# Attention scores of a hybrid encoder block on 64-row tiles of TensorE, without a padded copy of the keys

## The chip, the cores and the metric

The kernel runs on one core of a Trainium2 chip. The metric is the device time of one execution in microseconds (us). A core has five engines with an instruction queue each: TensorE (PE, the matrix array of 128 rows by 128 columns; a matmul contracts over the rows), VectorE (DVE), ScalarE (ACT), GpSimd (POOL) and SyncE (SP, which here only starts transfers). They run side by side and wait for each other on semaphores; each takes its own instructions strictly in the order in which they stand. SBUF is the memory on the core, 128 partitions wide; PSUM holds the results of matmuls in eight banks of 512 fp32 columns by 128 partitions.

## The reference

One layer of an encoder on 512 tokens of width 1024, all in fp32: a norm, one wide projection, attention and retention as two branches, gates, a merge, an output projection, and then a mixture of 64 experts. What the change touches is the attention: three groups of 8 heads, 64 numbers a head, rotary positions on queries and keys. Cut to that:

```python
ATTN_PAIRS = ((128, 1), (512, 4), (2048, 16))   # (window, dilation)
q_a = apply_rotary(q_a.reshape(B, S, n_a, HEAD_DIM), cos, sin)
k_a = apply_rotary(k_a.reshape(B, S, n_a, HEAD_DIM), cos, sin)
...
for g, (window, dilation) in enumerate(ATTN_PAIRS):
    o, l = dilated_window_attention(q_a[:, :, g], k_a[:, :, g], v_a[:, :, g], dilation, window // (2 * dilation))
...
    scores = jnp.einsum('nhbqd,nhbkd->nhbqk', qb, kw) * (Dh ** -0.5)
    scores = jnp.where(valid[None, None], scores, -jnp.inf)
    m = jnp.max(scores, axis=-1, keepdims=True)
    p = jnp.exp(scores - m)
    denom = jnp.sum(p, axis=-1, keepdims=True)
    out = jnp.einsum('nhbqk,nhbkd->nhbqd', p, vw) / denom
```

Group 0 looks at a block of 64 keys and its neighbours (192 keys a query block). Groups 1 and 2 look at every 4th or 16th token. The group outputs are summed, weighted by their denominators.

## The kernel before

**Projections.** The weights of the wide projection (w_in) come in pieces of 512 KB (`raw`), two buffers, loaded by SyncE (L109). ScalarE rounds each to a high half `wH` (L228) and VectorE takes the rest `wL` (L229), three buffers each. A product is then three matmuls: L293, L294 and L295 with the tokens in columns, L299, L300 and L301 with the weights in columns. They add up in the four `acc` banks of PSUM. All of this is called "projection" below; 0.233 us apart, these matmuls fill TensorE whenever nothing else stands in its queue.

**Keys and queries.** `rotary_to` takes a projected bank to SBUF (L331), copies it with the halves of each head swapped (`sw`, by DMA), and multiplies (VectorE L343, GpSimd L344). The sum of the two is done by GpSimd: in place for the queries (L346), and for the keys into `kP` (L350), a copy in which the two heads that share 128 partitions are set apart: head z keeps its 64 partitions in plane z, and the other 64 partitions of that plane hold zeros, put there once (L598).

**Scores.** Two heads share the 128 partitions, the first in partitions 0 to 63, the second in 64 to 127. With `kP`, one matmul over all 128 rows gives the scores of both heads: the zeros keep them apart. In group 0 (`windows`) a slot is such a pair of heads. For each of 4 tiles of 128 queries and each of 4 slots there are two matmuls (L640), one for each block of 64 queries; each fills 64 columns of the array and streams 2 x 192 keys into one PSUM bank. In groups 1 and 2 a half tile has 4 heads: two matmuls (L684) of 128 queries by 2 x 128 keys.

**Behind the scores.** `probs` lets VectorE add the mask and find the minimum (L604), and ScalarE take the exponential (L606). `transposed_probs` transposes by matmul into the same bank (L610), and VectorE copies to SBUF (L612). Matmuls with the values follow (AV: L650 and L655 in group 0, L696 in groups 1 and 2). ScalarE copies their banks into a record (L658, L698). Records of groups 1 and 2 go to DRAM (`scr`) and come back in the order of tokens (`rb`); `combine` weights and sums the three (L741, L744, L747) while the gate projections run. Four PSUM banks, `tmp`, serve scores, transposes and AV.

**Retention** stands ahead of the attention. Its scores (L546) are matmuls over 64 rows, with the two heads of a pair in PSUM banks of their own.

**Order.** The order in each engine's queue is fixed when the program is built, by a scheduler that follows the dependences and its own estimates of times; it mixes projections of what comes next between the attention's small matmuls. Behind the attention come four branch gates (`branch_gate`, evacuated by ScalarE at L715), the merge and the output projection. Then the experts: all 64 are streamed from memory in tiles of 2 MB (L981: `wa`, `wB`, `we`, `x`). The first of these, `we`, is loaded from ScalarE's queue; the SBUF it takes overlaps the end of group 0's record, so it waits for the last use of that record in `combine`.

## Time and profile before

| | |
|---|---|
| median of 3 runs | 1605.37 us (1605.3 to 1606.52) |
| profiled execution | 1605.17 us |
| its span, first to last instruction | 1603.3 us |
| busy: PE, DVE, ACT, POOL | 1337.7, 562.9, 316.0, 204.4 us |
| mean granted TensorE clock over the span | 0.917 |
| HBM read, written | 459.96 MB, 4.26 MB |

Busy shares are means over the span, and the span has stages with different limits, so they don't tell what bounds the kernel; that is read by stage. PE is a pipeline: one matmul's record overlaps the next one's, so the cost of a matmul in a stream is the distance from its start to the next start, not its duration. An fp32 matmul leaves two records. PEld, the loading of weights into the array, overlaps PE.

### The profile page before, as it was taken

The page shows a single profiled execution, that of the slowest core. Times are in us where ns is not written, and L with a number is a line of the kernel's source. Part 1 is how long each engine was busy: PE and PEld are TensorE (multiplying, and loading weights), DVE is VectorE, ACT ScalarE, POOL GpSimd, SP SyncE. Part 2 cuts the span into 40 slices and gives each one's busy share as a digit, 9 for nine tenths or more (in the row PEclk, how much of TensorE's full clock was granted, in tenths as well). Part 3 has the DMA queues.
Part 4 walks back from the last instruction along what each step waited for, and adds up shares of the span by engine and source line. Part 5 has one row for each costly group of instructions (what it writes and reads, how often), then busy time and mean ns, then how long its engine had stood idle before and what let it go on. Part 6 is the DMA issues. An engine that isn't in the chain of part 4 may idle for free.

```text
span 1603.3 us, 21137 instructions
## 1 busy us (share of the span) xinstructions
PE 1337.7 (83%) x8821; PEld 818.5 (51%) x8821; DVE 562.9 (35%) x1227; ACT 316.0 (20%) x605; POOL 204.4 (13%) x154
## 2 busy tenths in 40 slices
PE   8999999999999999998776776776686677677684
PEld 7788786697978788752331331332232232233133
DVE  7557564475847335541221121121021021022013
ACT  5332333334353423210000000000000000000002
POOL 2203352260715011000000000000000000000002
PEclk9999999999999999997997897998888887898887
DMA  4434253243434324999999999999999999999995
GB/s 168 123 92 106 93 145 93 56 121 105 113 108 155 123 92 176 376 409 427 429 428 428 427 430 426 428 427 430 426 428 430 427 428 430 426 428 428 428 428 238
DMA packets 70547, 476.14 MB, mean 297 GB/s; under 512 B 14192, under 2 KB 14320, under 8 KB 45680
## 3 DMA queue, kind: packets, MB, share of 16 engines
q1 hardware_dynamic: 68400, 471.46, 73.5%
q10 hardware_dynamic: 2048, 3.29, 0.6%
q8 instruction: 71, 1.16, 0.3%
q14 instruction: 28, 0.23, 0.0%
HBM read 459.96 MB, written 4.26 MB: 290 GB/s over the span
## 4 chain that ended last, share of the span: by engine, by line
PE 50%; DMA 39%; DVE 8%; issue 1%; ACT 1%; POOL 1%; SPq 0%; DVEq 0%; ACTq 0%; POOLq 0%
DMA wa<-in_moe_w2r_dram 14%; DMA x<-in_moe_w2r_dram 10%; DMA we<-in_moe_w2r_dram 9%; PE tmp L814 6%; PE acc L294 6%; PE acc L295 6%; PE acc L293 6%; PE acc L1018 5%; PE acc L300 3%; PE acc L301 3%; PE acc L299 3%; PE acc L1100 3%; PE tmp L1073 2%; DMA wa<-in_moe_w_dram 2%; DMA wB<-in_moe_w2c_dram 2%; DVE wL L229 2%
## 5 line engine op out<-in xcount | busy, mean ns | idle before, releaser
L1018 PE MATMUL acc<-wa,xT 128*32 128x512 f32 x1200 | 160.2, 669 | 74.5 <-DMA wa<-in_moe_w_dram 74.5
L229 DVE SCALAR_TENSOR_TENSOR wL<-raw,nwx,wH 128x512 fp32r<-128x512 f32 x152 | 150.7, 1025 | 104.2 <-ACT wH L228 102.7
L293 PE MATMUL acc<-x,wH 128*128 128x512 f32 x416 | 169.5, 407 | 1.1 <-ACT v L715 1.1
L295 PE MATMUL acc<-x,wL 128*128 128x512 f32 x416 | 167.4, 403 | 0.0
L294 PE MATMUL acc<-x,wH 128*128 128x512 f32 x416 | 167.0, 401 | 0.0
L228 ACT ACTIVATE wH<-raw,nwx 128x512 fp32r<-128x512 f32 x152 | 103.2, 717 | 173.7 <-PE acc L301 64.7
L299 PE MATMUL acc<-wH,x 128*128 128x512 f32 x320 | 127.7, 399 | 2.0 <-ACT rt L585 1.5
L1018 PEld LDWEIGHTS acc<-wa,xT 128*32 128x32 f32 x1200 | 36.1, 115 | 181.2 <-DMA wa<-in_moe_w_dram 92.9
L1100 PE MATMUL acc<-wa,hid 128*32 128x512 f32 x480 | 84.0, 834 | 52.1 <-DMA wa<-in_moe_w2r_dram 50.0
L301 PE MATMUL acc<-wH,x 128*128 128x512 f32 x320 | 127.1, 397 | 0.2 <-DVE x L216 0.2
L300 PE MATMUL acc<-wL,x 128*128 128x512 f32 x320 | 126.9, 397 | 0.0
L1160 POOL TENSOR_TENSOR wa<-big,wf 128x256 f32<-128x256 f32 x12 | 8.4, 733 | 899.0 <-DMA wB<-in_moe_w2c_dram 895.6
L1050 DVE SCALAR_TENSOR_TENSOR hid<-hid,gsl,acc 128x512 f32<-128x512 f32 x16 | 12.0, 747 | 303.2 <-ACT hid L1049 171.8
L814 PE MATMUL tmp<-oh,h 128*128 128x128 f32 x960 | 111.2, 277 | 0.3 <-DVE big L1084 0.3
L814 PEld LDWEIGHTS tmp<-oh,h 128*128 128x128 f32 x960 | 108.3, 192 | 4.7 <-DVE big L1084 4.7
L1063 DVE TENSOR_TENSOR yp<-acc,yp 128x512 fp32r<-128x512 f32 (+1 forms) x34 | 22.3, 656 | 245.8 <-ACT yp L1062 245.8
L293 PEld LDWEIGHTS acc<-x,wH 128*128 128x128 f32 x416 | 78.7, 189 | 21.2 <-issue 2.4
L295 PEld LDWEIGHTS acc<-x,wL 128*128 128x128 f32 x416 | 78.5, 189 | 19.9 <-issue 2.4
L294 PEld LDWEIGHTS acc<-x,wH 128*128 128x128 f32 x416 | 78.4, 188 | 18.6 <-issue 1.8
L1073 PE MATMUL tmp<-yp 128*128 128x512 f32 (+1 forms) x272 | 77.4, 421 | 4.6 <-ACT yp L1062 2.0
L1084 DVE TENSOR_TENSOR big<-big,tmp 128x512 f32<-128x512 f32 (+1 forms) x128 | 74.9, 646 | 16.0 <-PE tmp L1073 16.0
L299 PEld LDWEIGHTS acc<-wH,x 128*128 128x128 f32 x320 | 68.2, 213 | 13.7 <-ACT rt L585 2.4
(274 smaller groups left out, 1603.3 us busy)
## 6 DMA issues: line engine op xcount, KB each, us to landing
wa<-in_moe_w_dram SPq DMA_DIRECT2D x75, 2048.0 KB, 39.0
wa<-in_moe_w2r_dram SPq DMA_DIRECT2D x30, 2048.0 KB, 35.8
x<-in_moe_w_dram SPq DMA_DIRECT2D x25, 2048.0 KB, 39.1
raw<-in_w_in_dram SPq DMA_DIRECT2D x76, 512.0 KB, 3.6
x<-in_moe_w2r_dram SPq DMA_DIRECT2D x15, 2048.0 KB, 39.0
wB<-in_moe_w_dram SPq DMA_DIRECT2D x15, 2048.0 KB, 39.0
we<-in_moe_w2r_dram SPq DMA_DIRECT2D x10, 2048.0 KB, 38.4
we<-in_moe_w_dram SPq DMA_DIRECT2D x10, 2048.0 KB, 39.0
```

Of the source, the lines that this page charges most:

```text
L228: nc.scalar.activation(wH[:, k, :], raw[:, k, :], AF.Copy, scale=sc)
L229: nc.vector.scalar_tensor_tensor(wL[:, k, :], raw[:, k, :], sc, wH[:, k, :], op0=ALU.mult, op1=ALU.subtract)
L293: nc.tensor.matmul(ps[tt], wh[:, cs], srcH.blk(kt), **fl)
L294: nc.tensor.matmul(ps[tt], wh[:, cs], srcL.blk(kt), start=False, stop=False)
L295: nc.tensor.matmul(ps[tt], wl[:, cs], srcH.blk(kt), start=False, stop=(kt == nk - 1))
L299: nc.tensor.matmul(ps[tt], aH, wh, **fl)
L300: nc.tensor.matmul(ps[tt], aH, wl, start=False, stop=False)
L301: nc.tensor.matmul(ps[tt], aL, wh, start=False, stop=(kt == nk - 1))
L814: nc.tensor.matmul(gp[j // 4][:, (j % 4) * P:(j % 4 + 1) * P], h[:, t, j * P:(j + 1) * P], oh_t.rearrange("p e c -> p (e c)"), start=(t == ...
L1018: nc.tensor.matmul(p_[e * CAP:(e + 1) * CAP, :], xT[:, j, e * CAP:(e + 1) * CAP], wt[:, w_, e, :], start=(j == 0), stop=(j == NK - 1))
L1073: nc.tensor.matmul(pss[t], ohT[:, t * P:(t + 1) * P], y[:, cs], start=(i == 0), stop=(i == 1))
L1100: nc.tensor.matmul(py[hf][e * CAP:(e + 1) * CAP, :], hdT[:, i, e * CAP:(e + 1) * CAP], wt[:, e, hf * 512:(hf + 1) * 512], start=(i == 0), ...
```

## The change

`kP` and its zero fill go. The keys' rotary sum is done in place, like that of the queries. Scores are taken over the 64 rows of one head, by two 64-row tiles of the array, and the two heads of a pair write to PSUM banks of their own (`pair[0]`, `pair[1]`). In group 0 two slots share a pair of banks: 8 matmuls (quarters of the array, 192 keys each), then four heads' `probs`, and the transposes of each slot go back into one bank of the pair. In groups 1 and 2 a tile's 8 heads share a pair: 8 matmuls, `pair[i]` with the four heads of parity i; the record's copy (L705) becomes strided. The lines of after.py stand up to 10 lower or 8 higher than those of before: scores L635 and L686, probs L594 and L596, transposes L600, copy L602, AV L651, L656 and L703, gates L723, expert loads L989.

```diff
--- before.py
+++ after.py
@@ -342,12 +341,7 @@
                 w3 = w.rearrange("p (r l) -> p r l", r=4) if dilated else w
                 nc.vector.tensor_tensor(d3, d3, order(ropeT[:, 0, :]), op=ALU.mult)
                 nc.gpsimd.tensor_tensor(w3, w3, order(ropeT[:, 1, :]), op=ALU.mult)
-                if pad is None:
-                    (adder or nc.gpsimd).tensor_tensor(d, d, w, op=ALU.add)
-                else:
-                    for z in range(2):
-                        hp = slice(z * HD, (z + 1) * HD)
-                        nc.gpsimd.tensor_tensor(pad[hp, b - 1 + k, z, :], d[hp], w[hp], op=ALU.add)
+                (adder or nc.gpsimd).tensor_tensor(d, d, w, op=ALU.add)
         return evac
 
     def qk_tiles():
...
@@ -592,10 +586,6 @@
     scr = [dram.tile([S, REC], F32, name=f"scr{g}") for g in (1, 2)]
     at = right.enter_context(tc.tile_pool(name="at", bufs=1, side="right"))
     rec0 = at.tile([P, NT, REC], F32, name="rec0")
-
-    kP = at.tile([P, 4, 2, S], F32, name="kP")
-    for z in range(2):
-        nc.gpsimd.memset(kP[(1 - z) * HD:(2 - z) * HD, :, z, :], 0.0)
     orders = (nat, dil4, dil4)
 
     def probs(rec, hh, ps, sm, mask):
...
@@ -634,14 +625,24 @@
             po_ps = [tmp(), tmp()]
             for slot in range(4):
                 hh = 2 * slot
-                ps = tmp()
-                sm = rp.tile([P, 512], F32, name="sd", bufs=6)
-                for qs, k0 in parts_:
-                    nc.tensor.matmul(ps[qs, :2 * W], qT[:, slot, t * P + qs.start:t * P + qs.stop],
-                                     kP[:, slot, :, k0:k0 + W], start=True, stop=True)
-                for i in range(2):
-                    cs = slice(i * W, (i + 1) * W)
-                    probs(rec, hh + i, ps[:, cs], sm[:, cs], masks[:, mo_:mo_ + W])
+                if slot % 2 == 0:
+                    pair = [tmp(), tmp()]
+                    sms = []
+                    for u in range(2):
+                        for qs, k0 in parts_:
+                            for i in range(2):
+                                hp = slice(i * HD, (i + 1) * HD)
+                                nc.tensor.matmul(pair[i][qs, u * W:(u + 1) * W],
+                                                 qT[hp, slot + u, t * P + qs.start:t * P + qs.stop],
+                                                 kT[hp, slot + u, k0:k0 + W], start=True, stop=True)
+                    for u in range(2):
+                        sm = rp.tile([P, 512], F32, name="sd", bufs=6)
+                        sms.append(sm)
+                        for i in range(2):
+                            cs = slice(i * W, (i + 1) * W)
+                            probs(rec, hh + 2 * u + i, pair[i][:, u * W:(u + 1) * W], sm[:, cs],
+                                  masks[:, mo_:mo_ + W])
+                ps, sm = pair[slot % 2], sms[slot % 2]
                 prT = transposed_probs(ps, sm, 3)
                 oc = slice(slot * (HD + 1), (slot + 1) * (HD + 1))
                 for i in range(2):
@@ -661,7 +662,7 @@
     for g in range(3):
         qT, kT = qk_tiles()
         project_in(512 * g, None, rotary_to(qT, g > 0))
-        project_in(1536 + 512 * g, None, rotary_to(kT, g > 0, kP))
+        project_in(1536 + 512 * g, None, rotary_to(kT, g > 0))
         vt = rp.tile([P, 2080], F32, name="v", bufs=3)
         v4 = vt.rearrange("p (t h d) -> p t h d", t=NT, h=NH)
         nc.gpsimd.memset(v4[:, :, :, HD:HD + 1], 1.0)
...
         if g == 0:
-            windows(qT, v4)
+            windows(qT, kT, v4)
             continue
         for t in range(NT):
             rec_t = at.tile([P, REC], F32, name="rec", bufs=4)
             rec = rec_t[:, :]
-            for h0 in range(0, NH, 4):
-                ps = tmp()
+
+            ts = slice(t * P, (t + 1) * P)
+            pair = [tmp(), tmp()]
+            for x in range(4):
+                for i in range(2):
+                    hp = slice(i * HD, (i + 1) * HD)
+                    nc.tensor.matmul(pair[i][:, x * P:(x + 1) * P], qT[hp, x, ts], kT[hp, x, ts], start=True,
+                                     stop=True)
+            sms = []
+            for i in range(2):
                 sm = rp.tile([P, 512], F32, name="sd", bufs=6)
-                ts = slice(t * P, (t + 1) * P)
-                for i in range(0, 4, 2):
-                    nc.tensor.matmul(ps[:, i * P:(i + 2) * P], qT[:, (h0 + i) // 2, ts], kP[:, (h0 + i) // 2, :, ts],
-                                     start=True, stop=True)
-                for i in range(4):
-                    cs = slice(i * P, (i + 1) * P)
-                    probs(rec, h0 + i, ps[:, cs], sm[:, cs],
+                sms.append(sm)
+                for x in range(4):
+                    cs = slice(x * P, (x + 1) * P)
+                    probs(rec, 2 * x + i, pair[i][:, cs], sm[:, cs],
                           masks[:, 3 * HD:3 * HD + P] if g == 1 else masks[:, 9 * HD:])
-                prT = transposed_probs(ps, sm, 4)
+            for i in range(2):
+                prT = transposed_probs(pair[i], sms[i], 4)
                 po_ps = tmp()
-                for i in range(4):
-                    oc = i * (HD + 1)
+                for x in range(4):
+                    oc = x * (HD + 1)
                     for f in range(2):
-                        qs = slice(i * P + f * HD, i * P + (f + 1) * HD)
-                        nc.tensor.matmul(po_ps[f * HD:(f + 1) * HD, oc:oc + HD + 1], prT[:, qs], v4[:, t, h0 + i, :],
-                                         start=True, stop=True)
-                nc.scalar.copy(rec[:, h0 * (HD + 1):(h0 + 4) * (HD + 1)], po_ps[:, :4 * (HD + 1)])
+                        qs = slice(x * P + f * HD, x * P + (f + 1) * HD)
+                        nc.tensor.matmul(po_ps[f * HD:(f + 1) * HD, oc:oc + HD + 1], prT[:, qs],
+                                         v4[:, t, 2 * x + i, :], start=True, stop=True)
+                nc.scalar.copy(rec[:, :NH * (HD + 1)].rearrange("p (x z w) -> p x z w", x=4, z=2)[:, :, i],
+                               po_ps[:, :4 * (HD + 1)].rearrange("p (x w) -> p x w", x=4))
             nc.sync.dma_start(out=scr[g - 1].rearrange("(l r) c -> r l c", r=4)[t], in_=rec)
 
 
```

The change lets the scheduler order the queues anew up to the output projection; the first scores stand behind the same 414 projections as before. Three places.

TensorE, local stage, two successive slots of one tile of queries, before (L640 scores, L610 transposes, L650 and L655 AV, L293 to L295 projections):

```order
L640 MATMUL tmp<-kP,qT 64x384
L610 MATMUL tmp<-ident,sd 128x128 x3
L640 MATMUL tmp<-kP,qT 64x384
L295 MATMUL acc<-x_133,wL 128x512
L293 MATMUL acc<-x_133,wH 128x512
L294 MATMUL acc<-x_133,wH 128x512
L295 MATMUL acc<-x_133,wL 128x512
L650 MATMUL tmp<-v,sd 64x65 x4
L655 MATMUL tmp<-v,sd 64x65 x4
L640 MATMUL tmp<-kP,qT 64x384
L610 MATMUL tmp<-ident,sd 128x128 x3
L640 MATMUL tmp<-kP,qT 64x384
```

And now the beginning of a group of two slots (L635 scores, L600 transposes, L651 AV):

```order
L635 MATMUL tmp<-kT,qT 64x192 x8
L293 MATMUL acc<-x_132,wH 128x512
L294 MATMUL acc<-x_132,wH 128x512
L295 MATMUL acc<-x_132,wL 128x512
L293 MATMUL acc<-x_132,wH 128x512
L294 MATMUL acc<-x_132,wH 128x512
L295 MATMUL acc<-x_132,wL 128x512
L600 MATMUL tmp<-ident,sd 128x128 x4
L293 MATMUL acc<-x_133,wH 128x512
L600 MATMUL tmp<-ident,sd 128x128 x2
L294 MATMUL acc<-x_133,wH 128x512
L651 MATMUL tmp<-v,sd 64x65 x4
```

The transposes that stood between the two halves of a slot's scores stand behind six projections, and the scores of two slots stand together. Over the stage, before: 7 of the 16 slots have transposes between their two matmuls and 9 don't; 108 projections; 37 islands (unbroken stretches without a projection). Now: 8 groups of 8 score matmuls, 74 projections, 28 islands. The first group is followed by 13 projections, the others by 6.

TensorE, a dilated stage, a half of a tile of queries before (L684 scores, L610 transposes):

```order
L684 MATMUL tmp<-kP,qT 128x256 x2
L293 MATMUL acc<-x_132,wH 128x512
L294 MATMUL acc<-x_132,wH 128x512
L295 MATMUL acc<-x_132,wL 128x512
L293 MATMUL acc<-x_132,wH 128x512
L294 MATMUL acc<-x_132,wH 128x512
L295 MATMUL acc<-x_132,wL 128x512
L610 MATMUL tmp<-ident,sd 128x128 x3
L293 MATMUL acc<-x_132,wH 128x512
L610 MATMUL tmp<-ident,sd 128x128
L294 MATMUL acc<-x_132,wH 128x512
L295 MATMUL acc<-x_132,wL 128x512
```

And a tile now (L686 scores, L600 transposes):

```order
L686 MATMUL tmp<-kT,qT 128x128 x8
L295 MATMUL acc<-x_132,wL 128x512
L293 MATMUL acc<-x_132,wH 128x512
L294 MATMUL acc<-x_132,wH 128x512
L295 MATMUL acc<-x_132,wL 128x512
L293 MATMUL acc<-x_132,wH 128x512
L600 MATMUL tmp<-ident,sd 128x128 x3
L294 MATMUL acc<-x_132,wH 128x512
L600 MATMUL tmp<-ident,sd 128x128
L295 MATMUL acc<-x_132,wL 128x512
L600 MATMUL tmp<-ident,sd 128x128 x2
L293 MATMUL acc<-x_132,wH 128x512
```

Two blocks of scores with 6 to 10 projections behind each became one with 5 (in each stage's first tile 6), and the transposes of the second bank follow those of the first ahead of the first AV matmuls. Each of the two stages has 95 and 101 projections before and 55 now; the two together have 54 islands before and 48 now. The projections that left stand behind the stages: from the last AV matmuls of the second dilated stage to the next small matmuls there are 211 before and 257 now.

ScalarE, the load of `we` and what stands around it, before (L715 evacuates the second gate, `wH` is the rounding of weights; numbers tell buffers apart):

```order
L715 ACTIVATE kT_3973<-acc_3974,bg_63 128x512
L715 ACTIVATE kT_3973<-acc_3975,bg_63 128x512
L715 ACTIVATE kT_3973<-acc_3976,bg_63 128x512
L228 ACTIVATE wH_4217<-raw_4215,nwx_77 128x512
L715 ACTIVATE kT_3973<-acc_3977,bg_63 128x512
L228 ACTIVATE wH_4217<-raw_4215,nwx_77 128x512
L981 DMA we_5652<-in_moe_w13_dram 128x4096
L228 ACTIVATE wH_4261<-raw_4259,nwx_77 128x512 x2
```

And now (L723 is the gates' evacuation):

```order
L228 ACTIVATE wH_4125<-raw_4123,nwx_77 128x512 x2
L228 ACTIVATE wH_4178<-raw_4176,nwx_77 128x512 x2
L989 DMA we_5701<-in_moe_w13_dram 128x4096
L723 ACTIVATE kT_4022<-acc_4023,bg_63 128x512
L723 ACTIVATE kT_4022<-acc_4024,bg_63 128x512
L723 ACTIVATE kT_4022<-acc_4025,bg_63 128x512
L723 ACTIVATE kT_4022<-acc_4026,bg_63 128x512
L228 ACTIVATE wH_4222<-raw_4220,nwx_77 128x512 x2
L228 ACTIVATE wH_4266<-raw_4264,nwx_77 128x512 x2
```

The load stood behind the four evacuations of this gate; now it stands ahead of them, and two pieces of weights fewer are rounded ahead of it. On TensorE, 137 projections stand between the last AV matmul of the second dilated stage and the first matmul of the third gate, which takes a bank that the first of these evacuations empties; the first matmul with `wH_4222` stands 24 further on.

## Rows read from the trace of the kernel before

**Rows 1.** The page's slices: 40 equal slices of the span (40.1 us each); busy tenths of PE, the granted clock in tenths, busy tenths of the DMA engines, and GB/s.

```profile
span 1603.3 us, 21137 instructions
...
PE 8999999999999999998776776776686677677684
...
PEclk9999999999999999997997897998888887898887
DMA  4434253243434324999999999999999999999995
GB/s 168 123 92 106 93 145 93 56 121 105 113 108 155 123 92 176 376 409 427 429 428 428 427 430 426 428 427 430 426 428 430 427 428 430 426 428 428 428 428 238
```

**Rows 2.** Windows of the trace (the local stage, the first dilated stage, and all from 640 us on): stretch in us, its length, then busy time and instructions of PE, PEld, DVE, ACT and POOL, the granted clock, the DMA share and GB/s.

```profile
249.00:313.00 64.00, 64.00 (x479) 37.27 (x479) 27.91 (x92) 25.18 (x56) 5.04 (x5) 1.00 0.29 79
...
355.00:395.00 40.00, 40.00 (x290) 30.98 (x290) 18.23 (x80) 20.60 (x53) 2.44 (x2) 1.00 0.32 100
...
640.00:1604.00 964.00, 707.81 (x5498) 315.36 (x5496) 192.02 (x494) 68.16 (x153) 11.73 (x18) 0.86 0.98 417
```

**Rows 3.** Timeline of SyncE's queue around the start of the experts' stream: start and length in us, queue, line, transfer.

```profile
629.02 0.34 SPq L981 DMA_DIRECT2D wa<-in_moe_w_dram  x1
...
641.92 1.41 SPq L981 DMA_DIRECT2D wa<-in_moe_w_dram  x3
```

**Rows 4.** Groups of instructions by line and shape, from 140 to 620 us: line, engine, operation, tiles, partitions x elements, count, busy us, mean ns of one, idle time ahead.

```profile
L350 POOL TENSOR_TENSOR kP<-kT,sw 64x512 f32<-64x512 f32 x24 | 39.9, 1662 | 1.3
...
L346 POOL TENSOR_TENSOR qT<-qT,sw 128x512 f32<-128x512 f32 x12 | 20.5, 1725 | 4.8 <-issue 2.6 <-DVE qT L343 2.2
L606 ACT ACTIVATE sd<-sd,rec 128x128 f32<-128x128 f32 x64 | 20.5, 391 | 10.8 <-DVE rec L604 10.8
L640 PE MATMUL tmp<-kP,qT 128*64 128x384 f32 x64 | 18.9, 505 | 0.0
...
L606 ACT ACTIVATE sd<-sd,rec 128x192 f32<-128x192 f32 x32 | 12.8, 447 | 25.9 <-DVE rec L604 25.9
```

**Rows 5.** Timeline of PE in the local stage: start and length in us, line, tiles, shape, and how many records (two a matmul of fp32 scores).

```profile
257.25 1.51 PE L640 MATMUL tmp<-kP,qT 128*64 128x384 f32 x8
258.69 0.50 PE L293 MATMUL acc<-x,wH 128*128 128x512 f32 x1
259.03 0.39 PE L294 MATMUL acc<-x,wH 128*128 128x512 f32 x1
...
261.74 0.86 PE L640 MATMUL tmp<-kP,qT 128*64 128x384 f32 x2
262.53 0.55 PE L610 MATMUL tmp<-ident,sd 128*128 128x128 f32 x3
263.00 0.86 PE L640 MATMUL tmp<-kP,qT 128*64 128x384 f32 x2
263.79 0.50 PE L295 MATMUL acc<-x,wL 128*128 128x512 f32 x1
```

**Rows 6.** The same view in the first dilated stage.

```profile
369.16 0.40 PE L295 MATMUL acc<-x,wL 128*128 128x512 f32 x1
369.49 0.69 PE L696 MATMUL tmp<-v,sd 128*64 128x65 f32 x16
370.10 1.13 PE L684 MATMUL tmp<-kP,qT 128*128 128x256 f32 x4
370.88 0.58 PE L293 MATMUL acc<-x,wH 128*128 128x512 f32 x1
371.30 0.39 PE L294 MATMUL acc<-x,wH 128*128 128x512 f32 x1
...
372.23 0.40 PE L295 MATMUL acc<-x,wL 128*128 128x512 f32 x1
```

**Rows 7.** The same view in the retention, its scores and the projection behind them.

```profile
122.86 1.16 PE L546 MATMUL tmp<-kT 64*128 64x128 f32 x16
123.95 0.51 PE L299 MATMUL acc<-wH,x 128*128 128x512 f32 x1
```

**Rows 8.** Timeline of VectorE and of ScalarE behind the scores of rows 6.

```profile
371.27 0.29 DVE L604 CUSTOM_DVE_ANT_0 sd<-tmp,masks 128x128 f32<-128x128 f32 x1 [1.93 <-PE tmp L684]
...
371.49 0.28 DVE L604 CUSTOM_DVE_ANT_0 sd<-tmp,masks 128x128 f32<-128x128 f32 x1
...
371.67 1.28 ACT L606 ACTIVATE sd<-sd,rec 128x128 f32<-128x128 f32 x4 [1.07 <-DVE rec L604]
```

**Rows 9.** The chain of waits ahead of the second dilated stage: start and length in us, what.

```profile
434.48 7.38 DVE wL L229 x4
```

**Rows 10.** Timeline of PE in the third gate, where it waits; in brackets the idle time that the record shows ahead of it.

```profile
527.22 0.50 PE L293 MATMUL acc<-x,wH 128*128 128x512 f32 x1 [1.05 <-ACT v L715]
```

**Rows 11.** Timeline of ScalarE from the last dilated record copy to the load of `we`.

```profile
482.39 0.38 ACT L698 COPY rec<-tmp 128x260 f32<-128x260 f32 x1
...
504.82 0.71 ACT L228 ACTIVATE wH<-raw,nwx 128x512 fp32r<-128x512 f32 x1
514.82 0.33 ACTq L981 DMA_DIRECT2D we<-in_moe_w_dram  x1
```

**Rows 12.** The chain of waits behind that load.

```profile
515.36 8.52 DMA raw<-in_w_in_dram
```

More of the change, by code (lines that the diff above doesn't have):

```diff
@@ L321, in transposed, with rotary_to @@
         nc.scalar.copy(dst[:, :, tt * P:(tt + 1) * P], pt.rearrange("p (b t) -> p b t", b=4))
-    def rotary_to(dst, dilated, pad=None, adder=None):
+    def rotary_to(dst, dilated, adder=None):
         def order(v):
@@ L613, in transposed_probs, with windows @@
         return prT
-    def windows(qT, v4):
+    def windows(qT, kT, v4):
         W = 3 * HD
```

## The prediction

> **What bounds the kernel now.** I read the page's slices first. From the second slice to about 720 us PE is busy nine tenths or more, at a granted clock of nine tenths or more, while the DMA engines are two to five tenths busy in the first 16 slices (641 us) and nine tenths or more behind them, where they soon move 426 to 430 GB/s [rows 1]. So two limits follow each other: TensorE for the first 640 us, the stream of expert weights for the rest. The windows say it in numbers: in the local stage PE is busy for 64.00 of 64.00 us at clock 1.00 with 0.29 of the DMA engines, in the first dilated stage for 40.00 of 40.00 us, and behind 640 us the DMA share is 0.98 [rows 2]. SyncE's timeline shows the joint: the first expert load goes out at 629.02, and from 641.92 they go out back to back [rows 3]; ahead of them on that queue stand weight loads that wait for what TensorE has used up. What TensorE saves before 640 us moves the start of the stream, and so its end, by as much. The sum is made against the profiled execution (1605.17 us, span 1603.3), 0.2 us under the median of the runs (1605.37). No stage touched here is bound by anything but PE, so I price the change on PE's start-to-start times and then ask who is late next.
>
> **Local scores.** A slot (two heads) takes two matmuls of 384 columns, each on a 64-column half of the array. Its two halves run side by side when they are issued back to back: eight records, two slots, from 257.25 to 258.69, 1.44 us or 0.72 a slot. When three transposes stand between the halves, each half costs 0.79 alone (261.74 to 262.53, 263.00 to 263.79), 1.58 a slot [rows 5]. By the order 7 of 16 slots stand so and 9 do not: 7 x 1.58 + 9 x 0.72 = 17.5 us. (The 505 ns a record in the grouped row [rows 4] can't give this, since records overlap.) Now two slots are 8 matmuls of 192 columns, each on a quarter of the array. No row shows this form for scores. If four run at once, it is two turns of two passes of 192 columns; 1.44 us was 1536 such column steps one behind the other (two slots, two passes, 384), so 768 cost 0.72. The retention's scores, already 64-row tiles in two banks, take 1.09 us for 8 matmuls of 128 columns, two at a time (122.86 to 123.95) [rows 7], 1024 steps, and by that rate it is 0.82. If the row halves took turns after all, it would be 1.44. I take 0.78, near the two rows of the same kind: 8 x 0.78 = 6.2 us, and 11.3 us saved, of which the splits alone (7 x 0.86 = 6.0) are more than half.
>
> **Fewer turns between kinds of work.** A projection behind scores starts its successor after 0.34 us (258.69 to 259.03) and one ahead of AV matmuls after 0.33 (369.16 to 369.49), where four in a row take 0.93, 0.233 each (371.30 to 372.23) [rows 5, 6]. So each island of small matmuls costs 0.2 us beside its own time. The order has 37 islands in the local stage before and 28 now: 1.8 us. In the two dilated stages they fall from 54 to 48: 1.2 us. The Trainium skill, TensorEngine Tiling (Array Packing), section Key Properties, says that a change of tiling mode (not of tile) drains the engine; by that the new 64-row scores beside 128-row AV matmuls would pay more turns than the old ones. The rows show 0.1 us a turn, and the score of the old kind pays it too (0.42 behind L684).
>
> **Dilated scores.** A half of a tile of queries takes two matmuls of 256 columns, 0.78 us (370.10 to 370.88) [rows 6]; 16 halves in two stages are 12.5 us. Now a tile takes 8 matmuls of 128 columns on 64 rows, which is the retention's form with its 1.09 us [rows 7]: 8 x 1.09 = 8.7 us, 3.8 saved. With the islands it is 5.0 us. If the row tiles didn't overlap, it would be 2.0 a tile and 3.5 us lost.
>
> **What stays.** Transposes (112) and AV matmuls keep their count and form; the projections that no longer stand between scores move behind them, and cost the same there.
>
> **GpSimd and ScalarE.** 24 adds of 64 partitions, 39.9 us, become 12 of 128 in place, which for the queries take 1.725 us each, 20.7 us; 19 us of GpSimd's time go [rows 4], with the two fills. I cost that at nothing: PE has no idle time that the adds end. The record copies are now strided on ScalarE; at 0.38 us each [rows 11] they stand behind the last AV matmul of a tile.
>
> **New waits.** Before, a dilated half's scores were covered by 6 or more projections; now 8 scores are followed by 5 and the transposes. From the rows: the projection behind the scores starts at 370.88, VectorE's first mask at 371.27, the next 0.22 later (371.49), ScalarE's first exponential at 371.67, four in 1.28 [rows 8], so the third ends 0.39 + 0.40 + 0.96 = 1.75 us behind the scores. Five projections reach 1.28 us, two transposes 0.22 more, and the third waits some 0.25; later heads come at 0.32 each, about PE's pace. In a local group six projections end at 1.5 and the exponentials of 192 columns take 447 ns for 391 [rows 4]; again 0.2 to 0.4. I take 0.3 for each of 8 local and 8 dilated groups: 4.8 us lost; the ends are 0 and, with VectorE late, 1.8 (below).
>
> **ScalarE's queue.** The load of `we`, which waits for the last use of the combined record, stood behind the four gate evacuations; now it stands ahead of them, and behind it stand those and the next weight rounding; PE's next gate waits for their banks. Before, ScalarE was free from 505.5 on, and the load went out at 514.82, 32.4 us behind the last dilated record copy (482.39) [rows 11]. By the order 137 projections stand now between the end of the dilated stage and the first that needs such a bank: 137 x 0.233 = 32.0 us. So PE waits for the load, then an evacuation of 0.7: 1.5 to 2 us. The old stall there, 1.05 us at 527.22 [rows 10], came from a `raw` load issued at 515.36, behind `we`, that took 8.52 us [rows 12]; its turn has more room now and I let it go. Net 0.5 us lost, from 1.5 gained to 8 lost, as the combining runs shorter or longer.
>
> **Sum.** 11.3 + 1.8 + 5.0 = 18.1, less 4.8, less 0.5 = 12.8 us. 1605.2 - 12.8 = 1592.4; I say 1592. Its own range is 1585 (no waits, 0.72 a group, no stall) to 1599.
>
> **Rivals.**
> A: the row tiles don't run together. Then local groups cost 1.44 and dilated tiles 2.0; only splits and islands are saved: 17.5 - 11.5 + 3.0 - 3.5 = 5.5 us, less 2.5 for waits (which longer scores cover in part) and queue: 1602. Against it stand 16 records in 1.09 us [rows 7], whose serial time would be near 2. Chance 0.06.
> B: who evacuates becomes the bound. All four small PSUM banks are in use in a group (a pair and the AV pair), so scores, masks, exponentials, transposes and copy of one group run in a chain. If half of what the chain takes beyond its cover is seen, some 0.8 us in 16 groups, 12.8 us go: 18.1 - 12.8 - 0.5 = 4.8, 1600. PE's idle time before transposes in the grouped rows of before is small, which speaks against it. Chance 0.12. The Trainium skill, TensorEngine Tiling (Array Packing), section PSUM Bottleneck, states it as a rule: tiling speeds up TensorE and not the evacuation of PSUM, which may become the bottleneck; by it this rival is the likelier, and VectorE's busy 27.9 of 64 us [rows 2] is what I set against it.
> C, the slower side: VectorE is in a weight split whenever scores land. A split beside a busy GpSimd took 7.38 / 4 = 1.85 us [rows 9]. One such split between scores and masks in each of 16 groups costs 29.6 us: 1605.2 - 18.1 + 29.6 + 0.5 = 1617. It decides from 1.1 us a group on. In the local stage GpSimd hardly works, so splits are short there. Chance 0.04.
> D: the combining takes 10 us longer behind its loads, and ScalarE with its whole queue waits for it: 12.8 - 10 = 2.8, 1602. Chance 0.05. That the change saves nothing since the stream starts no sooner: 1605, chance 0.03; the saturated queue from 641.92 on, behind PE's own loads, speaks against it.
>
> **Numbers.** The forecast has 0.70. The range 1584 to 1603 takes in A, B and D; what is left out is C, the last case and part of the best ends. Faster or slower means by more than 0.2% (3.2 us, about what a measurement of this kernel tells from no change): faster holds the forecast, B and most of A and D, 0.87; same 0.08; slower 0.05.
>
> **What would show it.** The local stage is the window of 64 us [rows 2]: by the order 108 projections stand in it, 25.2 us, and 38.8 of other work; now 74 projections (17.3) and 38.8 - 13.1 + 2.4 = 28.1, so 45 us. Each dilated stage: 40 us with 95 projections (22.2); now 55 (12.8) and 17.8 - 2.5 + 1.2 = 16.5, so 29. The eight local scores: 0.72 to 0.82 from the first to the next projection, dilated ones 1.09; 1.44 or 2.0 would be A. Idle PE before transposes over 8 us in the three stages would be B or C, told apart by whether VectorE sits in splits. A PE gap of 1 to 2 us some 32 us behind the last dilated record copy is the queue's step; over 6 is D. The stream should saturate near 629 us in place of 641.9. I am wrong if the three stages shrink and that point doesn't move, or if they don't shrink.

## The result and the profile after

The changed kernel takes 1588.21 us, median of 4 runs (1587.59 to 1589.26), against 1605.34 before (1604.08 to 1606.52): 17.1 us less, a ratio of 0.9898 with an interval of 0.9886 to 0.991. The prediction was 1592, with a range of 1584 to 1603. The profiled execution took 1587.98 us, span 1585.9.

The page's slices show the same two limits as [rows 1], with the second one reached sooner: slice 16 already moves 248 GB/s, where it was 176.

```profile
span 1585.9 us, 21374 instructions
...
PE   9999999999999999997686677687687687677684
...
GB/s 170 124 93 107 94 145 88 90 119 107 127 143 148 91 93 248 370 423 429 427 427 429 428 428 428 428 428 429 426 428 429 428 428 428 428 428 429 426 428 245
```

SyncE's timeline gives the joint between them, which answers to [rows 3]: the first expert load goes out at 612.55, and from 625.44 they go out back to back, 16.5 us sooner than 641.92. The span is 17.4 us shorter. What PE saved came through to the end nearly one to one.

```profile
612.55 0.34 SPq L989 DMA_DIRECT2D wa<-in_moe_w_dram  x1
...
625.44 1.41 SPq L989 DMA_DIRECT2D wa<-in_moe_w_dram  x3
```

The windows of the three stages (stretch, length, then busy time and instructions of PE, PEld, DVE, ACT, POOL, the granted clock, DMA share, GB/s) answer to [rows 2]: 41.5 us for the local stage instead of 64, about 29 for each dilated stage, where the first had 40. Part of that is projections that now stand behind the stages, as the prediction's 45 and 29 have it. The clock is at its upper level in all three.

```profile
247.70:289.20 41.50, 41.50 (x508) 30.98 (x508) 23.47 (x88) 20.78 (x49) 0.25 (x2) 1.00 0.24 65
339.70:368.80 29.10, 28.04 (x281) 21.23 (x280) 16.84 (x79) 16.72 (x46) 0.00 (x0) 1.00 0.28 93
423.80:452.20 28.40, 28.06 (x281) 21.24 (x281) 17.38 (x79) 16.62 (x46) 2.16 (x2) 1.00 0.35 114
```

The two score blocks themselves, in PE's timeline (start and length, then line, tiles, shape and records). A local group takes 0.76 us (260.70 to 261.46), 0.38 a slot, where [rows 5] had 0.72 or 1.58; a dilated tile takes 1.09 us (347.96 to 349.05), where [rows 6] had 0.78 for a half. The sum had 0.78 and 1.09.

```profile
260.70 0.83 PE L635 MATMUL tmp<-kT,qT 64*64 64x192 f32 x16
261.46 0.50 PE L295 MATMUL acc<-x,wL 128*128 128x512 f32 x1
...
347.96 1.16 PE L686 MATMUL tmp<-kT,qT 64*128 64x128 f32 x16
349.05 0.50 PE L295 MATMUL acc<-x,wL 128*128 128x512 f32 x1
```

To see where the time went, I lined the two traces up by the number of projections that PE has started (counted from 0). Their count (2304) is the same, so the difference of the times at which both start the n-th is what has been won up to there:

| projection | where | won so far, us |
|---|---|---|
| 100 | start-up | 1.0 |
| 800 | ahead of the local stage | 1.3 |
| 1000 | behind it | 15.6 |
| 1300 | behind the first dilated stage | 16.8 |
| 1600 | behind the second | 19.5 |
| 1650 | first block of the third gate | 15.2 |
| 1740 | where the old stall was | 16.5 |
| 2300 | end of the projections | 16.7 |

The points 1000, 1300 and 1600 lie in the same piece of work in both kernels, between the stages. So the local stage gave 14.3 us, the dilated ones 1.2 and 2.6 (3.9 together), the third gate took back 4.3 and the old stall returned 1.3 of it; 1.3 us came from the start, where nothing was changed.

The third gate is the one place that got worse. ScalarE's timeline shows it, the rows that answer to [rows 11]:

```profile
475.40 1.34 ACT L228 ACTIVATE wH<-raw,nwx 128x512 fp32r<-128x512 f32 x2 [6.69 <-DMA raw<-in_w_in_dram]
485.65 0.34 ACTq L989 DMA_DIRECT2D we<-in_moe_w_dram  x1
486.04 2.42 ACT L723 ACTIVATE kT<-acc,bg 128x512 f32<-128x512 f32 x4 [9.30 <-issue]
```

From 476.7 on ScalarE does nothing; the load of `we` goes out at 485.65, and only then do the gate's four evacuations run. PE's timeline, in place of [rows 10]:

```profile
483.93 0.40 PE L295 MATMUL acc<-x,wL 128*128 128x512 f32 x1
486.78 0.50 PE L293 MATMUL acc<-x,wH 128*128 128x512 f32 x1 [2.46 <-ACT kT L723]
...
488.01 0.63 PE L294 MATMUL acc<-x,wH 128*128 128x512 f32 x1
488.43 0.63 PE L295 MATMUL acc<-x,wL 128*128 128x512 f32 x1
...
490.99 0.39 PE L295 MATMUL acc<-x,wL 128*128 128x512 f32 x1
491.23 0.39 PE L293 MATMUL acc<-x,wH 128*128 128x512 f32 x1
```

PE stands for 2.6 us (2.85 less one projection), and then eight matmuls start 0.43 us apart instead of 0.23. The windows say why: the granted clock falls from 1.00 to 0.57 on average between 487 and 491, which is time at 1.2 GHz mixed with time at 2.4, and is back at 1.00 behind it. The wait cost 2.6 us and the slow matmuls behind it another 1.6.

```profile
487.00:491.00 4.00, 4.00 (x12) 3.10 (x12) 1.90 (x3) 3.90 (x7) 0.00 (x0) 0.57 0.84 328
491.00:500.00 9.00, 9.00 (x40) 7.29 (x39) 2.26 (x4) 1.75 (x3) 0.00 (x0) 1.00 0.55 194
```

### The profile page after: what moved, and what is told of

It is laid out like the page before. It is cut to its first block, busy times and chain, and to the rows that moved or that the text cites. A ratio compares the mean times of both kernels' runs of the same rounds, so it can differ in the third digit from the quotient of the medians.

```text
span 1585.9 us, 21374 instructions
## 1 busy us (share of the span) xinstructions
PE 1318.5 (83%) x8949; PEld 818.0 (52%) x8949; DVE 559.3 (35%) x1227; ACT 312.5 (20%) x603; POOL 184.7 (12%) x140
## 4 chain that ended last, share of the span: by engine, by line
PE 52%; DMA 38%; DVE 7%; issue 2%; ACT 1%; POOL 1%; SPq 0%; DVEq 0%; ACTq 0%; POOLq 0%
DMA x<-in_moe_w2r_dram 12%; DMA wa<-in_moe_w2r_dram 11%; DMA we<-in_moe_w2r_dram 10%; PE tmp L822 7%; PE acc L294 6%; PE acc L295 6%; PE acc L293 6%; PE acc L1026 5%; PE acc L300 3%; PE acc L299 3%; PE acc L301 3%; PE tmp L1081 3%; PE acc L1108 2%; DMA wB<-in_moe_w2c_dram 2%; DVE wL L229 1%
## 5 line engine op out<-in xcount | busy, mean ns | idle before, releaser
L1026 PE MATMUL acc<-wa,xT 128*32 128x512 f32 x1200 | 165.2, 686 | 72.9 <-DMA wa<-in_moe_w_dram 72.9
L293 PE MATMUL acc<-x,wH 128*128 128x512 f32 x416 | 168.0, 404 | 2.5 <-ACT kT L723 2.5
L295 PE MATMUL acc<-x,wL 128*128 128x512 f32 x416 | 166.9, 401 | 0.0
L293 PEld LDWEIGHTS acc<-x,wH 128*128 128x128 f32 x416 | 78.9, 190 | 21.8 <-ACT kT L723 2.9
L295 PEld LDWEIGHTS acc<-x,wL 128*128 128x128 f32 x416 | 78.9, 190 | 18.4 <-issue 0.6
L1108 PEld LDWEIGHTS acc<-wa,hid 128*32 128x32 f32 x480 | 16.5, 133 | 117.9 <-issue 66.5
```

The costliest lines, as they stand in the source:

```text
L293: nc.tensor.matmul(ps[tt], wh[:, cs], srcH.blk(kt), **fl)
L295: nc.tensor.matmul(ps[tt], wl[:, cs], srcH.blk(kt), start=False, stop=(kt == nk - 1))
L1026: nc.tensor.matmul(p_[e * CAP:(e + 1) * CAP, :], xT[:, j, e * CAP:(e + 1) * CAP], wt[:, w_, e, :], start=(j == 0), stop=(j == NK - 1))
L1108: nc.tensor.matmul(py[hf][e * CAP:(e + 1) * CAP, :], hdT[:, i, e * CAP:(e + 1) * CAP], wt[:, e, hf * 512:(hf + 1) * 512], start=(i == 0), ...
```

## The experiments

**One part alone.** First the local stage without the dilated ones, and the other way round. In the first, `windows` and the call are as in the change and the keys of group 0 alone are summed in place; in the second, the dilated loop is as in the change and group 0 keeps `kP`.

```diff
-        project_in(1536 + 512 * g, None, rotary_to(kT, g > 0, kP))
+        project_in(1536 + 512 * g, None, rotary_to(kT, g > 0, kP if g else None))
...
-            windows(qT, v4)
+            windows(qT, kT, v4)
```

> Only the local stage is changed (64-row tiles, two slots a group); the dilated groups keep kP and their 128-row scores, and the load of we stays behind the gate's evacuations as before. Theory (three separate terms: local -14.3 us, dilated -4.0, the load of we +3.0, and 1.4 us of start-up that belongs to the run and not to the change): 1605.3 - 14.3 = 1591, local stage near 41 us, dilated stages unchanged at 39.4 and 41.5, PE gap of 1.45 in the third gate as before. Rival (the early 1.4 us is part of the change, from GpSimd or the memory layout): 1589.6. Rival (the dilated stages carry more than half): above 1595.

Measured: 1593.63 us against 1604.83, ratio 0.9928 (0.9912 to 0.9945), 11.2 us less where the theory had 14.3. Lined up by projections, the profiled execution (1589.66 us) has won 14.5 us behind the local stage and the same 14.5 at the end; the gate's load stands as before, and so does the old stall. The trace bears out the first term. The three runs without a trace took 1593.2 to 1594.4, some 4 us more than the profiled one, and where those 4 us lie stays open.

> Only the dilated stages are changed; the local stage keeps kP. By the order the load of we now stands ahead of the second gate's evacuations, as in the changed kernel. Theory: -4.0 in the two dilated stages, +3.0 in the gate (a PE gap near 2.85 us and slow matmuls behind it): 1604.3, so the dilated part alone gains almost nothing and the stages show it nevertheless (28 to 29 us each in place of 39.4 and 41.5). Rival (the load's place costs nothing net): 1601.3.

Measured: 1602.91 us, ratio 0.9986 (0.9977 to 0.9996). This lies between the theory (1604.3) and the rival (1601.3), and the time alone doesn't tell them apart. The trace does: from its first scores to the projection behind its last AV matmul, a dilated stage takes 28.2 and 29.1 us, 3.7 us are won behind both, and then comes the gate: a gap of 2.94 us, a loss of 4.4 with the slow matmuls, and 0.8 us won in the end. The part that works in its own stages gains next to nothing in the sum, as the load's place in ScalarE's queue takes it back. By the traces the two parts add up (14.5 and 0.8); by the medians they give 11.2 and 1.9, some 4 us less than the whole change, which is the open point above.

**Grouping or row tiles?** Two slots, or two halves of a tile, are scored together into two banks, but with `kP` and 128 rows:

```diff
+                if slot % 2 == 0:
+                    pair = [tmp(), tmp()]
+                    sms = []
+                    for u in range(2):
+                        for qs, k0 in parts_:
+                            nc.tensor.matmul(pair[u][qs, :2 * W], qT[:, slot + u, t * P + qs.start:t * P + qs.stop],
+                                             kP[:, slot + u, :, k0:k0 + W], start=True, stop=True)
...
```

The dilated loop is grouped in the same way.

> The grouping of the change (two slots, or two halves of a tile, score together into two banks) but with kP and 128-row scores. Theory (grouping ends the split slots, the 64-row tiles halve what is left): local scores 1.44 us a group against 0.78, so the local stage gains 6.0 + about 2 and not 14; dilated scores 1.56 a tile, no gain; the load of we costs 3: 1605.3 - 8 + 3 = 1600. Rival (all of the gain is grouping and fewer turns, the row tiles give nothing): 1588 to 1590, as the change. Rival (all of it is the row tiles): 1605 to 1608.

Measured: 1612.89 us, ratio 1.0045 (1.0028 to 1.0061): slower than before. The local stage did as the theory said: all eight groups take 1.44 us,

```profile
262.93 1.51 PE L642 MATMUL tmp<-kP,qT 128*64 128x384 f32 x8
264.37 0.50 PE L295 MATMUL acc<-x,wL 128*128 128x512 f32 x1
```

and 7.8 us are won behind it. That this is just the predicted 6.0 for splits and 1.8 for islands is chance: in this run's order the stage has 35 islands, two fewer than before and not nine, so that at 0.2 us each they explain 0.4, and some 1.4 us have no price in the sum. The change won 6.5 us more there: 5.4 from the scores (8 x 0.68), which are the row tiles, and about the rest from its seven fewer islands. In a dilated tile whose keys are there, the grouped scores take 1.64 us on 128 rows, against 1.09 on 64:

```profile
361.30 1.99 PE L689 MATMUL tmp<-kP,qT 128*128 128x256 f32 x8
362.94 0.59 PE L293 MATMUL acc<-x,wH 128*128 128x512 f32 x1
```

That is 4.4 us over eight tiles. But the dilated stages lost 6.5 each, which no theory had. PE's timeline shows the first tile's scores waiting twice for the keys:

```profile
347.49 1.02 PE L689 MATMUL tmp<-kP,qT 128*128 128x256 f32 x4
350.02 0.70 PE L689 MATMUL tmp<-kP,qT 128*128 128x256 f32 x2 [1.51 <-POOL kP L350]
352.67 1.22 PE L689 MATMUL tmp<-kP,qT 128*128 128x256 f32 x2 [1.95 <-POOL kP L350]
353.33 0.99 PE L293 MATMUL acc<-x,wH 128*128 128x512 f32 x1
```

Before, a half tile needed two slots of keys, and the second half came 13 projections later, while GpSimd was still adding. Scored together, a tile needs all four slots at once, and GpSimd's last add is late. So the step that costed GpSimd's part at nothing was in doubt.

**GpSimd's adds.** The change, with the keys' sum done in two adds of 64 partitions again; PE's order is that of the change.

```diff
+                if split:
+                    for z in range(2):
+                        hp = slice(z * HD, (z + 1) * HD)
+                        nc.gpsimd.tensor_tensor(d[hp], d[hp], w[hp], op=ALU.add)
+                else:
+                    (adder or nc.gpsimd).tensor_tensor(d, d, w, op=ALU.add)
...
```

> The change, with the keys' rotary sum done by GpSimd in two adds of 64 partitions again (24 instead of 12 instructions, 20 us more of GpSimd). Theory (GpSimd ends nowhere last): 1588.2, within 1 us. Rival (GpSimd's shorter work is part of the gain, through the keys' arrival or through VectorE's slower splits beside it): 1590 to 1593.

Measured: 1600.02 us (9 runs, 1597.65 to 1601.22), ratio 0.9971 (0.996 to 0.9981), and so some 12 us behind the change. My theory fell, and by more than the rival asked. The local stage is as in the change, and each dilated stage is over 5 us longer. It lies in the first tile, whose scores, begun at 339.70, now take 5.96 us in place of 1.09, and behind them PE runs at the lower clock for 3 us (granted 0.50 from 345.66 to 349):

```profile
341.94 0.48 PE L691 MATMUL tmp<-kT,qT 64*128 64x128 f32 x2 [1.19 <-POOL kT L347]
343.61 0.79 PE L691 MATMUL tmp<-kT,qT 64*128 64x128 f32 x2 [1.18 <-POOL kT L347]
344.94 0.79 PE L691 MATMUL tmp<-kT,qT 64*128 64x128 f32 x2 [0.54 <-POOL kT L347]
345.66 0.79 PE L293 MATMUL acc<-x,wH 128*128 128x512 f32 x1
```

GpSimd's timeline, of the change and of this run, for the last adds ahead of the first dilated stage:

```profile
335.29 3.44 POOL L344 TENSOR_TENSOR kT<-kT,sw 128x512 f32<-128x512 f32 x2
```

```profile
338.48 6.40 POOL L347 TENSOR_TENSOR kT<-kT,sw 64x512 f32<-64x512 f32 x4
```

In the change the last add ends at 338.7, one microsecond ahead of the first dilated scores (339.8); with half adds it ends at 344.9, 5 us behind them. PE, VectorE and ScalarE have the same order of instructions in both, so the adds in place are no by-product: they pay for scoring a whole tile at once.

**Do the row halves run together?** The change, with the score matmuls issued head by head, so that the lower 64 rows are through before the upper ones begin.

```diff
-                    for u in range(2):
-                        for qs, k0 in parts_:
-                            for i in range(2):
+                    for i in range(2):
+                        for u in range(2):
+                            for qs, k0 in parts_:
...
-            for x in range(4):
-                for i in range(2):
+            for i in range(2):
+                for x in range(4):
```

> The change with the score matmuls of a group issued head by head (all of the lower 64 rows, then all of the upper), everything else in the same order. Theory (row halves run at the same time only when they are issued next to each other): local group 1.44 us in place of 0.78 (+5.3 over 8), dilated tile about 2.0 in place of 1.09 (+7.3 over 8): 1588.2 + 12.6 = 1601, some 2 us less if waits behind the scores shrink. Rival (tiles overlap whatever the order, or PE reorders): 1588.

Measured: 1596.55 us, ratio 0.9942 (0.9925 to 0.9958). Neither theory holds. A local group takes 0.81 us against 0.76, so the theory's 1.44 is wrong; a dilated tile takes 1.64, between 1.09 and 2.0. (That 128-row scores took 1.64 too says nothing, as far as the runs show.)

```profile
353.77 1.71 PE L686 MATMUL tmp<-kT,qT 64*128 64x128 f32 x16
355.41 0.50 PE L293 MATMUL acc<-x,wH 128*128 128x512 f32 x1
```

The starts of the 16 records of that block and their lengths in ns show pairs 4 to 6 ns apart in the middle and single file at both ends:

```
353.775 373; 353.988 272; 354.100 272; 354.212 272; 354.323 272; 354.329 373; 354.435 272; 354.542 272;
354.547 272; 354.654 272; 354.658 272; 354.766 272; 354.877 272; 354.989 272; 355.101 272; 355.212 272
```

As I read it, the second record of 373 ns, at 354.329, is the first on the upper rows (the block's first record has that length too, and in the change the first two), so PE began on them while the lower rows still had records to come. The records that raise a semaphore fit that: each half has eight, and it is the eleventh (354.658) and the sixteenth that do. The Trainium skill, TensorE: Matmul & The Clock Gate, Part 3, says that matmuls start in strict program order and that tiles of different rows overlap; the overlap agrees with these rows, the strict order I can't reconcile with them, and here each fp32 matmul leaves two records. Of the 8 us, the scores are 4.8 (8 x 0.05 and 8 x 0.55). The rest goes with the new order: the scheduler put two projections behind most scores in place of five or six, and PE waits some 0.45 us ahead of the transposes in most local groups. My premise that everything else would keep its order was wrong.

**The load of `we`.** The change, with that load tied behind the third gate's last evacuation in ScalarE's queue:

```diff
-        (nc.scalar if nw[0] == 1 else nc.sync).dma_start(out=t_, in_=src)
+        if nw[0] == 1:
+            with tc.issue_after(gate_ins[11]):
+                nc.scalar.dma_start(out=t_, in_=src)
+        else:
+            nc.sync.dma_start(out=t_, in_=src)
...
```

> The change, with the first expert load (we) put on ScalarE's queue behind the third gate's evacuations. Theory (in the changed kernel ScalarE stands from 476.7 to 485.6 in front of that load, TensorE waits 2.6 us for the evacuation behind it and runs seven matmuls at 0.43 us instead of 0.23, some 4.2 us in all): the gap at the third gate goes, 1588.2 - 4 = 1584; a stall of up to 1.3 us may come back where a weight piece lands behind the 2 MB. Rival (the stall is covered by something later, the stream starts when it did): 1588.

> The change with the load of we behind the third gate's evacuations, again, on the chip of the run above. Theory (the queue step cost 4.2 us against a stall of 1.3 that came back in part elsewhere): 2.5 to 4 us under the changed kernel. Rival (the first measurement was the chip's): no difference beyond 0.5 us.

> The changed kernel a second time, beside the two below on the same chip. Expected: 1588.2 within 1 us. The 120th projection starts at 44.8 or at 46.2 us: at 44.8 again if the start-up gain belongs to the change, at either if it is a matter of the run.

Measured: 1585.7 us (ratio 0.9878, 0.986 to 0.9896) the first time. Beside the changed kernel on one chip, 1587.39 (0.989, 0.9873 to 0.9906) against 1588.67 (0.9897, 0.9881 to 0.9914). The medians give 2.5 and 1.3 us, the second neither the theory's 2.5 to 4 nor the rival's 0.5, and since the intervals overlap, the times alone don't exclude that it gains nothing. The traces say more. In the two executions of the changed kernel the gate's first block loses 4.3 us; in the two with the late load 0.6 and 0.7, and PE waits 0.3 and 0.4 us there instead of 2.5:

```profile
492.19 0.50 PE L293 MATMUL acc<-x,wH 128*128 128x512 f32 x1 [0.40 <-ACT kT L724]
```

At the end of the projections the late load is 1.4 us ahead in the first pair of traces and 2.4 in the second, and not 3.7. What takes the rest is the spread of runs, of which two parts could be found. One lies ahead of the first transposes of the two dilated stages, where PE waits for exponentials. The four traces have the same order in every queue up to there, and yet from one start to the next PE takes 1.46 and 0.73 us, then 1.45 and 1.34 in the changed kernel, and 2.92 and 1.51, then 1.96 and 1.52 with the late load; why, no run here tells. The other lies near the start. In the changed kernel's first trace the 120th projection starts at 44.81 us and in its second at 46.20, with nothing changed; in the first trace of the kernel before it starts at 46.22. Of the eleven traces besides that of before, four have it between 44.7 and 44.9, seven between 46.0 and 46.6, and the second one of the kernel before is among the latter (46.03):

> The kernel before, profiled a second time. Theory (the 1.4 us by which the changed kernel is ahead at the 120th projection, 45 us from the start, is a matter of the run): the time of the 120th projection falls anywhere between 44.8 and 46.3. Rival (it belongs to the change): 46.2 again, to 0.1 us.

The kernel before took 1604.94 us there, and its stages were the same to 0.5 us. Its 46.03 lies in the theory's range and 0.2 from the first trace's 46.22, so that it hardly tells theory and rival apart; what the second trace of the changed kernel shows is that the change doesn't always bring the early start. But the four early traces are all of kernels without `kP`, and all five traces with `kP` are late: whether the change makes the early start possible stays open. Without those 1.3 us the first pair of traces leaves 16.1 us of the span's 17.4. The second trace of the changed kernel, late as both of the kernel before, is 14.2 to 14.7 us shorter in span than they are, while the medians beside it differ by 16.5. GpSimd's timeline in the first and in the second trace of the changed kernel shows the two ways: eight products without a break, or a pause after each pair.

```profile
35.35 10.88 POOL L430 TENSOR_TENSOR qT<-rot,zeta 128x512 f32<-128x512 f32 x8 [16.27 <-DVE rot L426]
```

```profile
35.42 2.04 POOL L430 TENSOR_TENSOR qT<-rot,zeta 128x512 f32<-128x512 f32 x2 [16.32 <-DVE rot L426]
```

And VectorE's second `rot`, in the same two traces: 0.68 us or 1.55, beside the same GpSimd product, which takes 1.62 us in the first trace and 1.04 in the second. Which of the two comes first at that point is not the same in each run; why, no run here tells.

```profile
36.38 0.68 DVE L426 TENSOR_TENSOR rot<-rt,rt 128x512 f32<-128x512 f32 x1
```

```profile
36.46 1.55 DVE L426 TENSOR_TENSOR rot<-rt,rt 128x512 f32<-128x512 f32 x1
```

**Masks first.** What waiting was left behind the scores: in the changed kernel, 1.46 us from the last projection to the first transposes in the first dilated stage and 0.73 in the second. PE waits for an exponential there, and VectorE's masks stand behind a weight split that itself waited for ScalarE:

```profile
342.12 0.40 PE L295 MATMUL acc<-x,wL 128*128 128x512 f32 x1
343.58 0.62 PE L600 MATMUL tmp<-ident,sd 128*128 128x128 f32 x3 [1.06 <-ACT sd L596]
```

```profile
341.85 0.75 DVE L229 SCALAR_TENSOR_TENSOR wL<-raw,nwx,wH 128x512 fp32r<-128x512 f32 x1 [1.91 <-ACT wH L228]
342.51 0.28 DVE L594 CUSTOM_DVE_ANT_0 sd<-tmp,masks 128x128 f32<-128x128 f32 x1
```

On top of the late load, `probs` was given priority in the scheduler (`with tc.high_priority():` around its two instructions).

> The same with the masks and exponentials given priority in the scheduler; the order then has 7 or 8 projections between dilated scores and the first transposes instead of 5 or 6, and fewer islands. Theory (what is left of waiting behind scores is 1.5 us in the first tile of each dilated stage and little elsewhere): 1 to 3 us under the run above. Rival (VectorE's queue still has the weight splits ahead of the masks, and the stalls stay): the same time.

Measured: 1585.9 us, ratio 0.9883 (0.9866 to 0.9899); 1.5 under the late load beside it, within the spread. In the trace the first tiles still wait (1.06 and 1.34 us between two starts), with the weight splits still ahead of the masks, as the rival had it; but the gate loses only 0.3 us, and lined up by projections this execution ends 3.2 us ahead of the changed kernel's first one, with the same early start-up. The three medians with the late load (1585.7, 1587.4, 1585.9) lie under both of the changed kernel (1588.2, 1588.7).

## Why the prediction was right

- **One to one into the stream:** right. 16.5 us at the first back-to-back loads, 17.4 in the span.
- **Local scores, 11.3 us, and islands, 1.8:** the scores are right in mechanism and size: 0.76 a group against 0.78, and 1.44 a group on 128 rows, as taken for rival A. The stage gave 14.3 against 13.1 without waits. The islands' price wasn't tested by itself: with 35 islands in place of 28, the grouped kernel with 128 rows still won 7.8 us.
- **Dilated scores, 3.8, and islands:** 1.09 us a tile, as the retention's rows said. The stages gave 3.9 us net, waits included; 5.0 less 2.4 of waits had been predicted. That the keys would be there for a whole tile at once was not asked.
- **New waits, 4.8 us:** this is the term that was mis-sized most. PE's waits ahead of transposes come to 1.7 us (1.46 and 0.73, less a projection each) and lie in the first tile of each dilated stage; the local groups wait for nothing. The kernel before waited in such a place too, 0.96 us from start to start in its second dilated stage:

```profile
443.57 0.33 PE L610 MATMUL tmp<-ident,sd 128*128 128x128 f32 x1 [0.57 <-ACT sd L606]
```

  So about 1 us is new, and 5.0 less 1.0 is close to what the dilated stages gave. I had taken VectorE's lag behind the scores, 0.39 us, from the old form. In the new one the first mask starts 0.10 us behind the projection that follows the scores (349.05), the eight exponentials take 2.45 us, and the third is through before the fifth projection is:

```profile
349.15 0.29 DVE L594 CUSTOM_DVE_ANT_0 sd<-tmp,masks 128x128 f32<-128x128 f32 x1 [1.93 <-PE tmp L686]
...
349.49 2.45 ACT L596 ACTIVATE sd<-sd,rec 128x128 f32<-128x128 f32 x8 [1.03 <-DVE rec L594]
```

- **ScalarE's queue, 0.5 us:** the place and the cause were right, and the price was 3.0 (4.3 less 1.3 of the old stall). The load went out 33.5 us behind the last dilated record copy (452.20 to 485.65), against 32.4 taken, which is one part; the other is the lower clock behind the gap, which I hadn't counted.
- **GpSimd at nothing:** right in its sum by luck, and wrong in its reason. I had looked only at whether PE had idle time that shorter adds would end. The question was whether the change needs the shorter adds, and it does: without them it is 12 us slower, and with them the last add ends just 1 us ahead of the first dilated scores.
- **Rival A** fell with 0.76 and 1.09. **B** and **C** fell in the stages: a split stands between scores and masks in three of 16 groups, and in the local one of these 13 projections cover it. **D** didn't happen: the load went out 1 us later behind the record copy than taken and not 10, and PE's gap of 2.6 us is nearer to the sign of the queue's step (1 to 2) than to D's (over 6).

By places, measured less predicted gain in the two profiled executions: local stage 3.6 us (2.4 of it waits that didn't come), dilated stages 1.3, start-up 1.3, third gate -2.5, and 0.7 behind the last projection, 4.4 in all: 1592.4 was the sum, 1587.98 the profiled execution. Terms missed in both directions, so that part of the nearness is luck; and the 1.3 us near the start don't come in every run.

## What to carry to other kernels

Price small matmuls from their start-to-start distance in the form in which they will stand, and look for an existing stage with that form: two such rows gave the new scores to 3% here. When work is grouped so that it needs more of its inputs at once, ask of each input when its last part comes, and what the change has done to that; an engine that was never waited for can become the late one. And a transfer that waits in a compute engine's queue holds everything behind it: its price is the wait of whoever needs that engine, with whatever slow matmuls follow the wait.

## What was not expected of the hardware

GpSimd needed as long for 64 partitions as for 128: 1.66 us for an add of 64x512 [rows 4] and 1.70 for one of 128x512 in the changed kernel.

```profile
L344 POOL TENSOR_TENSOR kT<-kT,sw 128x512 f32<-128x512 f32 x12 | 20.2, 1701 | 0.0
```

A PE gap of some 2.5 us at the third gate, behind a stretch in which PE was never idle, is followed by seven or eight matmuls at the lower clock in five of the six traces that have it, both of the changed kernel among them (the second has a granted clock of 0.66 over 488 to 493); in the changed kernel they cost 1.6 us more. It isn't a rule. With the two adds none was slow behind that gap (2.45 us at 497.47), and the gate then lost 2.7 us in place of 4.3. And in the first trace with the late load PE stood as long in the first dilated stage, with the clock at 1.00 behind it; what decides, no run here tells.

```profile
345.18 0.62 PE L600 MATMUL tmp<-ident,sd 128*128 128x128 f32 x3 [2.52 <-ACT sd L596]
```

The two halves of the array's rows overlapped in part even when their matmuls were issued one half behind the other: by the reading above, three of eight records of the upper rows had begun before the last of the lower. The section on the cores says that each engine takes its instructions strictly in order; for the starts of those matmuls this run shows otherwise.
